# Scratch layout of the split state-space operands: one write of each half, and loads that repeat rows

## The chip, the cores and the metric

The kernel runs on one core of a Trainium2 chip. The metric is the device time of one launch in microseconds (us); before the change it is 2741.55 us, the median of 3 runs (2741.41 to 2743.21). PE is the matrix engine, DVE the vector engine, ACT the scalar engine, POOL the GpSimd engine, SP the engine that issues the weight transfers.

## The reference, cut to what matters

A trunk of two layers over 256 tokens of width 2048, all in float32. Each layer has a mixer (differential attention beside a state-space branch, both gated) and an MLP. The change touches only the input side of the state-space branch:

```
u   = x @ w_in[:, OFF_U:OFF_GA]                      # (256, 1024): 64 groups of 16 channels
z   = (exp(dt a) - 1) / a                            # complex, per group and state
bb  = z * b                                          # (64 groups, 64 states, 16 channels), complex
bu  = einsum('blgh,gph->blgp', u, bb)                # re and im
s_t = exp(dt a) s_(t-1) + bu_t                       # scanned over the 256 tokens
y   = Re(c s) + d u, then GELU, then a sigmoid GLU
```

The kernel moves z to the output side (into c), so that the product it forms is u with the plain b.

## The kernel before, in words

**Weights.** All large products have the weights streamed: SP issues one transfer of 512 KB for each chunk of 256 rows (line 344, four buffers for the raw data). ACT rounds the chunk to the upper part `whi` (line 142) and DVE forms the rest `wlo` (line 144), three buffers each. PE multiplies in float32r and sums three products: upper by upper, upper by lower, lower by upper (lines 532 to 534 for the projections, 457 to 461 for products by token, 555 for the MLP's first half).

**The state-space branch in the background.** `ssm_gen` (line 643) is a generator of small steps that are put between the chunks of the large products; a scheduler then sets the order on each engine from its own estimate of durations. The product bu is made in 32 steps, 16 a layer (4 groups g of feature tiles, 4 steps k each). Every step takes one tile `bs` (weights: upper and lower part of b) and one tile `us` (upper and lower part of u), both with a single buffer, and issues 4 matmuls into `bu` (line 685), 128 states by 256 tokens each. u is in the order of its channels, and a step needs the channels of one pair of groups on 96 partitions: 32 rows, three times, so that one matmul with 96 rows sums upper by upper, lower by upper and upper by lower. This regrouping goes through memory:

- `b_gen` (line 572) loads the raw b (`braw`, line 577), splits it into `hi` and `lo` for each of four g, and writes each part to the scratch tensor `bsplit`: three writes of 256 KB per g (hi, lo, hi again; line 590), 12 a layer.
- `u_evac` (line 927) runs four times a layer, after each half of the two u products; it splits its two feature tiles and writes three parts to `usplit` (hi, hi, lo; line 934), 256 KB each, 12 a layer.
- `operands(i)` (line 657) loads `bs` and `us` of step i (lines 662 and 664), 192 KB each. It is called right after the matmuls of step i-1, whose reading frees the two buffers.

All of these transfers are issued by POOL, in order. A write takes 128 partitions of 2 KB; its target is a view of three dimensions, 4 blocks of 32 rows, since each part has its own place between the blocks. Other POOL transfers of the same size (`emem`, `xkeep`, `lnb`, `cz`) have 128 rows as the first dimension on both sides.

After the bu matmuls, DVE multiplies by the powers e (lines 692 to 698), scans (line 710), and PE forms y (line 731).

Of the kernel before, what the change touches and what calls it, by code (L numbers as in the profile page):

```python
# [11 lines left out]
F32 = mybir.dt.float32  # L12
F32R = mybir.dt.float32r
# [7 lines left out]
P = 128  # L21
# [9 lines left out]
L = 64  # L31
# [73 lines left out]
def trunk(ctx: ExitStack, tc: tile.TileContext, A, out):  # L105
# [13 lines left out]
    def nm(s):  # L119
        uid[0] += 1  # L120
        return f"{s}_{uid[0]}"

    def slot(shape, dt=F32, name="slot"):
        return slots.tile(shape, dt, tag="slot", name=nm(name))
# [447 lines left out]
    def b_gen(l):  # L572


        raw = slot([P, 4, 2, 256], name="braw")
        for g in range(4):
            hold(GP.dma_start(raw[:, g], A["bT"][l][:, g]))
            yield 0.3
        if l == 0:
            yield from ssm_param_gen()  # L580
        else:
            yield 2.0
        bsplit[l] = dram.tile([4, 4, 3, 32, 2, 256], F32, tag=f"bsplit{l}", name=f"bsplit{l}")
        hi, lo = (slot([P, 4, 2, 256], name="bhl") for _ in range(2))
        for g in range(4):
            h = SC.activation(hi[:, g].bitcast(F32R), raw[:, g], AF.Copy)
            hold(h)
            V.tensor_tensor(lo[:, g].bitcast(F32R), raw[:, g], hi[:, g], op=ALU.subtract)
            for m, t in enumerate((hi, lo, hi)):
                GP.dma_start(bsplit[l][g, :, m], t[:, g])  # L590
            yield 0.6

    def e_steps(l, g, im, re, hold=lambda i: i):
        jj = slice(l * 32 + 8 * g, l * 32 + 8 * g + 8)
# [48 lines left out]
    def ssm_gen(l, st):  # L643
        lp = l * 32
        e_re = slot([P, 4, 8, L], name="e_re")
        e_im = slot([P, 4, 8, L], name="e_im")
        w = [slot([P, NCH, 8, L], name="sw") for _ in range(2)]
        for g in range(4):
            if l in emem:
                for t, e in zip((e_re, e_im), emem[l]):  # L650
                    drip.append((t[:, g], e[:, g]))
            else:
                for step in e_steps(l, g, e_im[:, g], e_re[:, g]):
                    yield 0.1 if isinstance(step, tuple) else step
        while st["u"] is None:
            yield 0.5
        def operands(i):
            if i == 16:
                return None
            g, h, kk = i // 4, i // 2 % 2, i % 2  # L660
            bs = tmp.tile([96, 2, 2, P], F32, tag="bs", name=nm("bs"), bufs=1)
            GP.dma_start(bs.rearrange("p q c s -> p q (c s)"), bsplit[l][g, 2 * kk:2 * kk + 2, :, :, h].rearrange("q m r s -> (m r) q s"))
            us = tmp.tile([96, 2, 256], F32, tag="us", name=nm("us"), bufs=1)
            GP.dma_start(us, st["split"][2 * kk:2 * kk + 2, :, :, 2 * g + h].rearrange("q m r t -> (m r) q t"))
            return bs, us

        nxt = operands(0)
        uT = st["u"]
        for g in range(4):
            jj = slice(lp + 8 * g, lp + 8 * g + 8)  # L670
            cz = tmp.tile([P, 2, 8, 32], F32, tag="cz", name=nm("cz"), bufs=2)
            GP.dma_start(cz, cmem[l][g] if l in cmem else A["cT"][l, g])
            rt = t_bg([P, 8, L])
            SC.activation(rt, s_r[:, jj, None].broadcast_to([P, 8, L]), AF.Copy)
            GP.memset(rt[:, :, 0:1], 0.0)
            yield 0.1
            if l not in cmem:
                c_steps(l, g, cz)
                yield 2.0
            for k in range(4):  # L680
                bs, us = nxt
                bu = psa.tile([P, 2, 2, NCH, L], F32, tag="bu", name=nm("bu"), bufs=1)
                for q in range(2):
                    for ri in range(2):
                        PE.matmul(bu[:, q, ri].rearrange("p a b -> p (a b)"), bs[:, q, ri, :].bitcast(F32R), us[:, q, :].bitcast(F32R), start=True, stop=True)
                nxt = operands(4 * g + k + 1)
                yield 0.3
                er = e_re[:, g, 2 * k:2 * k + 2, None, :].broadcast_to([P, 2, NCH, L])
                ei = e_im[:, g, 2 * k:2 * k + 2, None, :].broadcast_to([P, 2, NCH, L])
                wr, wi = (w[ri][:, :, 2 * k:2 * k + 2, :].rearrange("p c q t -> p q c t") for ri in range(2))  # L690
                ta, tb = t_bg([P, 2, NCH, L]), t_bg([P, 2, NCH, L])
                V.tensor_tensor(wr, bu[:, :, 0], er, op=ALU.mult)
                V.tensor_tensor(ta, bu[:, :, 1], ei, op=ALU.mult)
                V.tensor_tensor(wi, bu[:, :, 1], er, op=ALU.mult)
                yield 1.8
                V.tensor_tensor(tb, bu[:, :, 0], ei, op=ALU.mult)
                V.tensor_tensor(wr, wr, ta, op=ALU.add)
                V.tensor_tensor(wi, wi, tb, op=ALU.subtract)
                yield 1.8
            rg = rt.rearrange("p a b -> p (a b)")  # L700
            er, ei = e_re[:, g], e_im[:, g]
            carry = None
            for c in range(NCH):
                if c > 0:
                    for ri in range(2):
                        V.tensor_tensor(carry[:, ri, :], carry[:, ri, :], s_r[:, lp + 8 * g:lp + 8 * g + 8], op=ALU.mult)
                        V.tensor_tensor(w[ri][:, c, :, 0], w[ri][:, c, :, 0], carry[:, ri, :], op=ALU.add)
                for ri in range(2):
                    wv = w[ri][:, c].rearrange("p a b -> p (a b)")
                    V.tensor_tensor_scan(wv, rg, wv, 0.0, ALU.mult, ALU.add)  # L710
                yield 2.4
                s = [w[0][:, c], w[1][:, c]]
                ta, tb, td = t_bg([P, 8, L]), t_bg([P, 8, L]), t_bg([P, 8, L])
                V.tensor_tensor(ta, s[1], ei, op=ALU.mult)
                V.tensor_tensor(tb, s[0], ei, op=ALU.mult)
                V.tensor_tensor(td, s[0], er, op=ALU.mult)
                yield 1.8
                V.tensor_tensor(s[1], s[1], er, op=ALU.mult)
                V.tensor_tensor(s[0], td, ta, op=ALU.subtract)
                V.tensor_tensor(s[1], s[1], tb, op=ALU.add)  # L720
                if c < NCH - 1:
                    carry = sm([P, 2, 8], tag="carry", bufs=2)
                    for ri in range(2):
                        V.tensor_copy(carry[:, ri, :], s[ri][:, :, L - 1])
                yield 1.8
            yps = psa.tile([P, 2, 2, 256], F32, tag="bu", name=nm("y"), bufs=1)[:, 0]
            mm = [Chain() for _ in range(4)]
            for h in range(2):
                for ri in range(2):
                    for j in range(4):  # L730
                        mm[j](PE.matmul(yps[32 * j:32 * j + 32, h, :], cz[:, ri, 4 * h + j, :], w[ri][:, :, 4 * h + j, :],
                                        start=ri == 0, stop=ri == 1, tile_position=(0, 32 * j)))
            yield 0.3
            y, a = t_bg([P, 2, 256]), t_bg([P, 2, 256])
            uc = uT[:, 2 * g:2 * g + 2, :]
            for k in range(2):
                SC.activation(y[:, k, :], uc[:, k, :], AF.Copy, scale=dsk[:, l, 2 * g + k:2 * g + k + 1])
            V.tensor_tensor(y, yps, y, op=ALU.add)
            SC.activation(a, y, AF.Square, scale=math.sqrt(GELU_C))
            yield 0.7  # L740
            V.scalar_tensor_tensor(a, a, 1.0, y, op0=ALU.add, op1=ALU.mult)
            SC.activation(a, a, AF.Tanh, scale=GELU_K)
            yield 0.7
            V.scalar_tensor_tensor(uc, a, 1.0, y, op0=ALU.add, op1=ALU.mult)
            yield 0.6
# [165 lines left out]
    for l in range(DEPTH):  # L911
# [9 lines left out]
        sgen = early()  # L921
        first = False
        uT = slot([P, 8, 256], name="uT")
        uhl = [slot([P, 8, 256], name="uhl") for _ in range(2)]
        st["split"] = dram.tile([4, 3, 32, 8, 256], F32, tag=f"usplit{l}", name=f"usplit{l}")

        def u_evac(b, ps):
            ct = 4 * n + 2 * b
            u = uT[:, ct:ct + 2, :]
            hi, lo = (t[:, ct:ct + 2, :] for t in uhl)  # L930
            SC.activation(u, ps, AF.Copy)
            split(hi.bitcast(F32R), lo.bitcast(F32R), u)
            for m, t in enumerate((hi, hi, lo)):
                GP.dma_start(st["split"][:, m, :, ct:ct + 2], t)

        rate[0] = RATE[l]
        bg.add(sgen)
# [237 lines left out]
```

## Time and profile before

| | |
|---|---|
| median of 3 runs | 2741.55 us |
| the profiled execution's own time | 2731.09 us |
| its span, first to last instruction | 2729.3 us |
| PE busy | 2676.5 us (98%) |
| DVE busy | 1908.7 us (70%) |
| ACT busy | 1312.6 us (48%) |
| POOL busy | 147.1 us (5%) |
| moved by SP's queue | 482.40 MB, 53.2% of the 16 DMA engines' span |
| moved by POOL's queue | 50.99 MB, 6.6% |
| mean granted TensorE clock | 0.994 |

The profile gives each engine's busy time and, for each group of instructions, the idle time before them and what ended it. A wait of PE's in the chain adds to the span; idle time of an engine that nobody waits for adds nothing. For transfers it gives the time from the issue to the landing. The 53.2% and 6.6% are shares of what the 16 DMA engines could do over the whole span, a mean over stretches that differ.

### The profile page before, as it was taken

Reading aid. Unit: us, or ns where it says so; the run is one execution under the profiler, and the core shown is the slowest. Engines: PE = TensorE matmul, PEld = TensorE weight load, DVE = VectorE, ACT = ScalarE, POOL = GpSimd, SP = SyncE. Lnnn points to the kernel's source line nnn. Section 1 sums busy time; section 2 is a strip of 40 time slices with the busy share of each in tenths; the row PEclk is TensorE's granted clock in tenths of the full one; section 3 lists DMA queues with packets and bytes.
Section 4 is the critical chain, followed back from the end, with each engine's and each line's share of the span. In section 5 each row is a group of like instructions: output and inputs, shape, how many; then the busy total and the mean of one; then the engine's idle time right before and its main releaser. Section 6 shows DMA issues by size and latency. Waiting matters only on the chain. (4 is left out here: it accounts for less than half of the span.)

```text
span 2729.3 us, 41597 instructions
## 1 busy us (share of the span) xinstructions
PE 2676.5 (98%) x16384; PEld 2371.8 (87%) x16384; DVE 1908.7 (70%) x2675; ACT 1312.6 (48%) x1755; POOL 147.1 (5%) x274
## 2 busy tenths in 40 slices
PE   7999999999999999999999999999999999999997
PEld 7889999988888888888789899999788888888876
DVE  6899988676765566655657998987776655556555
ACT  4554555454554454443444555544445544435442
POOL 3100000000000010000012000001000000000000
PEclk9999999999999999999999999999999999999999
DMA  8755555663655676655657555557746555555573
GB/s 262 224 187 188 174 173 169 212 234 122 220 190 192 205 237 212 220 198 195 227 167 253 185 179 171 166 179 230 252 135 205 187 194 191 190 195 186 193 234 121
DMA packets 158675, 536.04 MB, mean 196 GB/s; under 512 B 27504, under 2 KB 27536, under 8 KB 158480
## 3 DMA queue, kind: packets, MB, share of 16 engines
q1 hardware_dynamic: 133344, 482.40, 53.2%
q0 software_dynamic: 25136, 50.99, 6.6%
q8 instruction: 128, 2.10, 0.3%
q14 instruction: 67, 0.55, 0.1%
HBM read 513.32 MB, written 19.92 MB: 195 GB/s over the span
## 5 line engine op out<-in xcount | busy, mean ns | idle before, releaser
L144 DVE TENSOR_TENSOR wlo<-w,whi 128x1024 fp32r<-128x1024 f32 (+1 forms) x884 | 1078.3, 1221 | 660.3 <-ACT whi L142 655.3
L142 ACT ACTIVATE whi<-w 128x1024 fp32r<-128x1024 f32 (+1 forms) x884 | 934.3, 1058 | 1085.3 <-PE g L461 425.6
L555 PE MATMUL g<-xT,whi 128*128 128x512 f32 x1920 | 655.7, 395 | 2.3 <-ACT whi L142 2.3
L532 PE MATMUL g<-xT,whi 128*128 128x256 f32 x1792 | 509.3, 287 | 11.8 <-ACT whi L142 11.8
L533 PE MATMUL g<-xT,whi 128*128 128x256 f32 x1792 | 508.5, 286 | 0.0
L534 PE MATMUL g<-xT,wlo 128*128 128x256 f32 x1792 | 500.0, 287 | 7.1 <-DVE wlo L144 7.0
L555 PE MATMUL g<-xT,wlo 128*128 128x256 f32 x1920 | 497.7, 280 | 0.2 <-DVE wlo L144 0.2
L555 PEld LDWEIGHTS g<-xT,whi 128*128 128x128 f32 x1920 | 344.9, 188 | 66.9 <-ACT whi L142 2.6
L458 PE MATMUL g<-wlo,hT 128*128 128x512 f32 x972 | 379.4, 390 | 3.6 <-DVE wlo L144 3.5
L555 PEld LDWEIGHTS g<-xT,wlo 128*128 128x128 f32 x1920 | 362.1, 189 | 21.7 <-DVE wlo L144 1.4
L457 PE MATMUL g<-whi,hT 128*128 128x512 f32 x972 | 379.1, 390 | 0.9 <-ACT whi L142 0.9
L532 PEld LDWEIGHTS g<-xT,whi 128*128 128x128 f32 x1792 | 347.9, 194 | 14.7 <-ACT whi L142 12.9
L534 PEld LDWEIGHTS g<-xT,wlo 128*128 128x128 f32 x1792 | 341.8, 194 | 10.2 <-DVE wlo L144 9.6
L533 PEld LDWEIGHTS g<-xT,whi 128*128 128x128 f32 x1792 | 347.9, 194 | 1.0 <-issue 0.8
L461 PE MATMUL g<-whi,hT 128*128 128x512 f32 x972 | 300.3, 390 | 0.0
L458 PEld LDWEIGHTS g<-wlo,hT 128*128 128x128 f32 x972 | 182.7, 188 | 43.9 <-DVE wlo L144 5.7
L457 PEld LDWEIGHTS g<-whi,hT 128*128 128x128 f32 x972 | 182.9, 188 | 39.6 <-ACT whi L142 2.1
L461 PEld LDWEIGHTS g<-whi,hT 128*128 128x128 f32 x972 | 182.9, 188 | 38.0
L458 PE MATMUL g<-wlo,merged 128*128 128x512 f32 x216 | 85.3, 395 | 3.4 <-DVE wlo L144 3.2
L560 ACT ACTIVATE at<-g 128x256 f32<-128x256 f32 x120 | 43.8, 384 | 87.3 <-PE g L555 87.3
L457 PE MATMUL g<-whi,merged 128*128 128x512 f32 x216 | 84.4, 391 | 0.0
L710 DVE TENSOR_TENSOR_SCAN sw<-ss,sw 128x512 f32<-128x512 f32 x64 | 75.7, 1212 | 0.0
(290 smaller groups left out, 3186.1 us busy)
## 6 DMA issues: line engine op xcount, KB each, us to landing
w<-in_w_mlp_down_dram SPq DMA_DIRECT2D x256, 512.0 KB, 3.3
w<-in_w_in_dram SPq DMA_DIRECT2D x255, 512.0 KB, 3.4
w<-in_w_mlp_up_dram SPq DMA_DIRECT2D x240, 512.0 KB, 3.3
w<-in_w_out_dram SPq DMA_DIRECT2D x64, 512.0 KB, 4.3
w<-in_w_attn_up_dram SPq DMA_DIRECT2D x32, 512.0 KB, 3.3
w<-in_w_ssm_up_dram SPq DMA_DIRECT2D x32, 512.0 KB, 4.3
w<-in_w_glu_dram SPq DMA_DIRECT2D x16, 512.0 KB, 3.2
w<-in_w_mlp_head_dram SPq DMA_DIRECT2D x16, 512.0 KB, 3.5
```

The source lines that it names most:

```text
L142: SC.activation(hi, src, AF.Copy, scale=scale)
L144: V.tensor_tensor(lo, src, hi.bitcast(F32), op=ALU.subtract)
L457: mm(PE.matmul(ps[tt], act(kt)[:, 0, ts], hi[:, k, :], start=kt == 0, stop=False))
L458: mm(PE.matmul(ps[tt], act(kt)[:, 0, ts], lo[:, k, :], start=False, stop=False))
L461: mm(PE.matmul(ps[tt], act(kt)[:, 1, ts], hi[:, k, :], start=False, stop=kt == nkt - 1))
L532: m(PE.matmul(o, wh, ah, start=first and b % 2 == 0, stop=False))
L533: m(PE.matmul(o, wh, al, start=False, stop=False))
L534: m(PE.matmul(o, wl, ah, start=False, stop=last and b % 2 == 1))
L555: mm[j](PE.matmul(o, wt, mv, start=kt == 0 and i == 0, stop=last and i == 1))
L560: SC.activation(r[:, j], ps[j][:, 0, :], AF.Copy)
L710: V.tensor_tensor_scan(wv, rg, wv, 0.0, ALU.mult, ALU.add)
```

## The change

Each part of b and of u is now written once. Two groups g of b share one tile and one write of 1 MB (2 a layer), and each of the two u products ends in one write of 1 MB. The scratch tensors have the two parts of a row side by side: 4 blocks, 32 rows, 2 parts, and then 8 KB less the parts, so that a write is 128 rows of 8 KB that follow each other. A step's operands are now one block j of 32 rows, both parts: 64 rows. The load of `bs` takes these 64 rows twice (a first dimension of 2 that repeats), the load of `us` takes each row twice, in two transfers, one for each part. So a step has 128 partitions with four products (lower by lower too), 256 KB each of `bs` and `us`, three loads in place of two; the two feature tiles that a step yields are now k and k+4 in place of 2k and 2k+1.

```diff
@@ b_gen
-        bsplit[l] = dram.tile([4, 4, 3, 32, 2, 256], F32, tag=f"bsplit{l}", name=f"bsplit{l}")
-        hi, lo = (slot([P, 4, 2, 256], name="bhl") for _ in range(2))
-        for g in range(4):
-            h = SC.activation(hi[:, g].bitcast(F32R), raw[:, g], AF.Copy)
-            hold(h)
-            V.tensor_tensor(lo[:, g].bitcast(F32R), raw[:, g], hi[:, g], op=ALU.subtract)
-            for m, t in enumerate((hi, lo, hi)):
-                GP.dma_start(bsplit[l][g, :, m], t[:, g])
-            yield 0.6
+        bsplit[l] = [dram.tile([4, 32, 2, 2, 2, 256], F32, tag=f"bsplit{l}{i}", name=f"bsplit{l}{i}") for i in range(2)]
+        for i in range(2):
+            hl = slot([P, 2, 2, 2, 256], name="bhl")
+            for k in range(2):
+                hold(SC.activation(hl[:, 0, k].bitcast(F32R), raw[:, 2 * i + k], AF.Copy))
+                V.tensor_tensor(hl[:, 1, k].bitcast(F32R), raw[:, 2 * i + k], hl[:, 0, k], op=ALU.subtract)
+                yield 0.6
+            GP.dma_start(bsplit[l][i].rearrange("j r m k h c -> (j r) (m k h c)"), hl.rearrange("p m k h c -> p (m k h c)"))
@@ operands
-            g, h, kk = i // 4, i // 2 % 2, i % 2
-            bs = tmp.tile([96, 2, 2, P], F32, tag="bs", name=nm("bs"), bufs=1)
-            GP.dma_start(bs.rearrange("p q c s -> p q (c s)"), bsplit[l][g, 2 * kk:2 * kk + 2, :, :, h].rearrange("q m r s -> (m r) q s"))
-            us = tmp.tile([96, 2, 256], F32, tag="us", name=nm("us"), bufs=1)
-            GP.dma_start(us, st["split"][2 * kk:2 * kk + 2, :, :, 2 * g + h].rearrange("q m r t -> (m r) q t"))
+            g, j = i // 4, i % 4
+            bs = tmp.tile([P, 2, 2, P], F32, tag="bs", name=nm("bs"), bufs=1)
+            us = tmp.tile([P, 2, 256], F32, tag="us", name=nm("us"), bufs=1)
+            b = bsplit[l][g // 2][j, :, :, g % 2].rearrange("r m h c -> (r m) (h c)")
+            GP.dma_start(bs.rearrange("p h c s -> p (h c s)"), b[None].broadcast_to([2, 64, 512]))
+            for m in range(2):
+                u = st["split"][g // 2][j, :, m, 2 * (g % 2):2 * (g % 2) + 2].rearrange("r h t -> r (h t)")
+                GP.dma_start(us[64 * m:64 * m + 64].rearrange("p h t -> p (h t)"), u[:, None].broadcast_to([32, 2, 512]))
@@ the step's first DVE operations
-                er = e_re[:, g, 2 * k:2 * k + 2, None, :].broadcast_to([P, 2, NCH, L])
-                ei = e_im[:, g, 2 * k:2 * k + 2, None, :].broadcast_to([P, 2, NCH, L])
-                wr, wi = (w[ri][:, :, 2 * k:2 * k + 2, :].rearrange("p c q t -> p q c t") for ri in range(2))
+                er = e_re[:, g, k::4, None, :].broadcast_to([P, 2, NCH, L])
+                ei = e_im[:, g, k::4, None, :].broadcast_to([P, 2, NCH, L])
+                wr, wi = (w[ri][:, :, k::4, :].rearrange("p c q t -> p q c t") for ri in range(2))
@@ u_evac and its tiles
-        uhl = [slot([P, 8, 256], name="uhl") for _ in range(2)]
-        st["split"] = dram.tile([4, 3, 32, 8, 256], F32, tag=f"usplit{l}", name=f"usplit{l}")
+        uhl = [slot([P, 2, 4, 256], name="uhl") for _ in range(2)]
+        st["split"] = [dram.tile([4, 32, 2, 4, 256], F32, tag=f"usplit{l}{i}", name=f"usplit{l}{i}") for i in range(2)]
...
-            hi, lo = (t[:, ct:ct + 2, :] for t in uhl)
+            hi, lo = (uhl[n][:, m, 2 * b:2 * b + 2] for m in range(2))
...
-            for m, t in enumerate((hi, hi, lo)):
-                GP.dma_start(st["split"][:, m, :, ct:ct + 2], t)
+            if b == 1:
+                GP.dma_start(st["split"][n].rearrange("j r m c t -> (j r) (m c t)"), uhl[n].rearrange("p m c t -> p (m c t)"))
```

The scheduler places the instructions anew. The rows below stand in the built programs, engine by engine; the line numbers of the changed kernel are one less or two more than those of the kernel before. The last part of a row is the shape of what is written.

POOL in layer 0, at the loads of the first two steps. Before:

```order
L590 DMA bsplit_506<-bhl_508 4x32x512
L662 DMA bs_881<-bsplit_506 96x2x256
L590 DMA bsplit_506<-bhl_508 4x32x512
L664 DMA us_883<-usplit_170 96x2x256
L934 DMA usplit_170<-uhl_168 4x32x512 x4
L934 DMA usplit_170<-uhl_169 4x32x512 x2
L662 DMA bs_933<-bsplit_506 96x2x256
L664 DMA us_935<-usplit_170 96x2x256
```

Now, from the first write of b (the first write of u stands right ahead of it):

```order
L590 DMA bsplit_507<-bhl_509 128x2048
L590 DMA bsplit_508<-bhl_554 128x2048
L666 DMA us_864<-usplit_170 64x1x512 x2
L663 DMA bs_863<-bsplit_507 128x1x512
L663 DMA bs_916<-bsplit_507 128x1x512
L666 DMA us_917<-usplit_170 64x1x512 x2
L936 DMA usplit_171<-uhl_169 128x2048
```

Ahead of the first step's last load there stood 18 writes (12 of b, 6 of u); there stand 3 now. The second half of u was written between the loads of the two steps and is written behind both now.

PE in layer 0, about the first bu matmuls (`g` is a large product; rows with xT_118 are the first chunk of the product after u, with xT_141 a later one). Before:

```order
L532 MATMUL g_849<-xT_141,whi_944 128x256
L533 MATMUL g_849<-xT_141,whi_944 128x256
L532 MATMUL g_850<-xT_141,whi_944 128x256
L533 MATMUL g_850<-xT_141,whi_944 128x256
L685 MATMUL bu_928<-us_883,bs_881 128x256 x4
L534 MATMUL g_849<-xT_141,wlo_945 128x256
```

Now:

```order
L534 MATMUL g_520<-xT_163,wlo_750 128x256
L532 MATMUL g_831<-xT_118,whi_788 128x256
L533 MATMUL g_831<-xT_118,whi_788 128x256
L532 MATMUL g_832<-xT_118,whi_788 128x256
L533 MATMUL g_832<-xT_118,whi_788 128x256
L687 MATMUL bu_911<-us_864,bs_863 128x256 x4
L534 MATMUL g_831<-xT_118,wlo_789 128x256
```

The first bu matmuls stood behind 76 matmuls of the product after u; they stand behind 4 now, 72 matmuls earlier.

POOL in layer 1, about the first write of u (`xkeep` is the residual, put aside). Before:

```order
L447 DMA xkeep<-x_6005 128x512
L934 DMA usplit_12946<-uhl_12944 4x32x512 x2
L934 DMA usplit_12946<-uhl_12945 4x32x512 x2
L447 DMA xkeep<-x_6005 128x512 x3
L664 DMA us_13856<-usplit_12946 96x2x256
L447 DMA xkeep<-x_6006 128x512 x4
L934 DMA usplit_12946<-uhl_12944 4x32x512 x4
```

Now:

```order
L447 DMA xkeep<-x_6003 128x512
L936 DMA usplit_12935<-uhl_12933 128x2048
L447 DMA xkeep<-x_6003 128x512 x2
L666 DMA us_13835<-usplit_12935 64x1x512 x2
L447 DMA xkeep<-x_6003 128x512
L447 DMA xkeep<-x_6004 128x512 x4
L663 DMA bs_13849<-bsplit_9753 128x1x512
```

One write stands where six stood ahead of the first load of `us`, and the second write of u is behind the loads of the second step here too.

In PE's row, the other matmuls between the bu matmuls of one step and of the next number, for steps 1 to 15 of layer 0: before 159, 33, 72, 499, 64, 29, 30, 413, 90, 54, 53, 478, 89, 58, 50; now 226, 38, 72, 499, 64, 29, 36, 414, 96, 60, 56, 477, 85, 63, 55. For steps 17 to 31 of layer 1: before 106, 66, 48, 579, 47, 29, 48, 458, 86, 136, 51, 458, 74, 56, 56; now 59, 82, 59, 540, 50, 13, 36, 499, 135, 123, 60, 465, 57, 59, 61. (Steps are counted from 0; the counts take single matmuls of whatever width.)

## Rows read from the trace of the kernel before

**Rows 1.** Page, part 1: busy us (share of the span) xinstructions.

```profile
PE 2676.5 (98%) x16384; PEld 2371.8 (87%) x16384; DVE 1908.7 (70%) x2675; ACT 1312.6 (48%) x1755; POOL 147.1 (5%) x274
```

**Rows 2.** Windows: start:end, length, busy by engine, PE clock, DMA share, GB/s.

```profile
200.00:300.00 100.00, 100.00 (x741) 91.91 (x740) 93.56 (x167) 51.12 (x97) 8.33 (x14) 1.00 0.57 185
300.00:400.00 100.00, 100.00 (x819) 94.87 (x818) 91.52 (x163) 49.87 (x91) 5.20 (x9) 1.00 0.53 174
```

**Rows 3.** Waits from 40 to 100 us, those of PE: total, times, longest.

```profile
PE bu L685 <- DMA us<-usplit: 5.0, 1, 5.0
...
PE g L532 <- ACT whi L142: 3.9, 1, 3.9
...
PE g L534 <- DVE wlo L144: 1.9, 3, 0.9
```

**Rows 4.** Waits of PE from 900 to 1500 us.

```profile
PE g L555 <- ACT whi L142: 2.3, 1, 2.3
PE bu L685 <- DMA us<-usplit: 1.4, 2, 1.3
```

**Rows 5.** Windows of 5 us, in the order of engines of rows 2.

```profile
60.00:65.00 5.00, 0.91 (x4) 0.50 (x2) 1.05 (x1) 1.80 (x2) 1.87 (x4) 0.75 0.97 308
65.00:70.00 5.00, 4.77 (x25) 4.78 (x26) 4.08 (x10) 2.99 (x5) 2.02 (x3) 0.57 0.95 250
```

**Rows 6.** Timeline of POOL, layer 0: start, us, what, idle before and its end.

```profile
68.13 0.67 POOL L662 DMA_DIRECT2D bs<-bsplit  x1 [0.92 <-DMA usplit<-uhl]
...
73.51 0.67 POOL L664 DMA_DIRECT2D us<-usplit  x1 [1.62 <-DMA bsplit<-bhl]
```

**Rows 7.** Page of transfers: issues, KB each, median us from issue to landing.

```profile
bsplit<-bhl POOLq DMA_DIRECT2D x24, 256.0 KB, 12.7
usplit<-uhl POOLq DMA_DIRECT2D x24, 256.0 KB, 12.9
bs<-bsplit POOLq DMA_DIRECT2D x32, 192.0 KB, 3.8
...
emem<-ss POOLq DMA_DIRECT2D x8, 256.0 KB, 4.7
...
e_re<-emem POOLq DMA_DIRECT2D x4, 256.0 KB, 4.0
```

**Rows 8.** The tile bhl: landing of the writes of b.

```profile
DMA to landing us min/median/max: 7.0/12.7/18.3
```

**Rows 9.** Narrow windows after the first bsplit write of layer 1, and of emem writes.

```profile
953.90:954.40 0.50, 0.50 (x5) 0.41 (x4) 0.14 (x2) 0.42 (x2) 0.35 (x1) 1.00 0.43 26
990.00:990.50 0.50, 0.50 (x4) 0.40 (x3) 0.00 (x0) 0.50 (x2) 0.12 (x1) 0.50 1.09 344
990.50:991.00 0.50, 0.50 (x3) 0.40 (x3) 0.00 (x0) 0.50 (x1) 0.22 (x1) 0.61 0.94 377
```

**Rows 10.** Timeline of POOL at steps 5 to 7 of layer 0.

```profile
205.07 0.64 POOL L662 DMA_DIRECT2D bs<-bsplit  x1 [13.88 <-PE bu L685]
205.71 0.64 POOL L664 DMA_DIRECT2D us<-usplit  x1
212.15 0.64 POOL L662 DMA_DIRECT2D bs<-bsplit  x1 [5.81 <-PE bu L685]
```

**Rows 11.** Timeline of PE there, and the pace of matmuls with 512 columns.

```profile
211.21 0.64 PE L685 MATMUL bu<-us,bs 96*128 96x256 f32 x4
211.69 0.40 PE L458 MATMUL g<-wlo,xT 128*128 128x512 f32 x1
211.93 0.40 PE L457 MATMUL g<-whi,xT 128*128 128x512 f32 x1
...
218.08 0.72 PE L685 MATMUL bu<-us,bs 96*128 96x256 f32 x4
```

**Rows 12.** Timeline of PE: the pace of matmuls with 256 columns.

```profile
20.09 0.28 PE L534 MATMUL g<-xT,wlo 128*128 128x256 f32 x1
20.21 0.28 PE L532 MATMUL g<-xT,whi 128*128 128x256 f32 x1
```

## The prediction

> **What bounds the kernel now.** I read the page's busy times first: PE is busy for 98% of the span [rows 1], so a change gains only what PE waits, and loses whatever it makes PE wait. The windows say where the other engines come near: from 200 to 400 us, where the steps of the state-space branch run, PE is busy throughout, DVE for 92 to 94%, and the DMA engines for 53 to 57%, nearly all of it weights [rows 2]. There PE has no wait left that could cover a new one. Next come PE's waits. Between 40 and 100 us it waits 10.8 us: 5.0 us, once, for the load of `us`, and 3.9 and 1.9 us for weights that are split late [rows 3]. In layer 1, from 900 to 1500 us, it waits 2.3 us for a late weight and 1.4 us for `us` [rows 4]. A wait costs more than its length: with PE's wait of 3.9 us the granted clock is 0.75 and then 0.57 in the two windows from 60 us [rows 5], means of stretches at 2.4 and at 1.2 GHz, and that is (0.25 + 0.43) x 5 = 3.4 us of PE's pace. The first loads of operands are late because POOL's row is full of writes: `bs` goes out at 68.1 us and `us` at 73.5, after waits for earlier writes [rows 6].
>
> **The writes.** They are slow now. The median landing is 12.7 and 12.9 us, though others of this size that have 128 rows first on both sides, `emem`, take 4.7 [rows 7]; the best write of b still takes 7.0 [rows 8], so a crowded queue is not all of it. The narrow windows show the difference: just after the first write of b in layer 1 the engines move 26 GB/s at a share of 0.43; with two writes of `emem` and the weights they move 344 and 377 GB/s [rows 9]. I read this as the shape: a transfer whose one side leads with a dimension of 4 runs on few of the 16 engines. One engine moves 377 / (16 x 0.94) = 25 GB/s [rows 9], so 256 KB take 2.6 us on four engines and 0.65 us on sixteen.
>
> The change removes 48 such writes, 12.6 MB, and adds 8 of 1 MB, 8.4 MB, with 128 rows first on both sides. A 1 MB write is not in the trace: at the 377 GB/s of rows 9 it takes 2.8 us, at the pace of a crowded `bsplit` write it would take four times 12.7 us. I take it near the first, since the form is that of `emem`. What this gives is bounded by PE's waits where writes run. In layer 0 these are the 10.8 us of rows 3 and, for its two long waits, twice 3.4 us of clock; in layer 1 the 3.7 us of rows 4 and, if each of two places costs half of what rows 5 show, 3.4 us: 25 us at most, and 0 at least. I take 8. In layer 0 the first bu matmuls now stand 72 matmuls earlier, 8.6 us at 0.12 us each [rows 12]; three writes of 1 MB and then the loads still stand ahead of them, so PE waits there again: 4 us of gain. In layer 1 one write replaces six ahead of the first load: 4 us.
>
> **The loads.** This is where I expect the change to lose. Each of 32 steps loads `bs` and `us` right after the bu matmuls of the step before, and PE needs both at the next bu. One step from the rows: bu ends at 211.85 us, `bs` is issued at 212.15, `us` 0.64 later (as at 205.07 and 205.71) [rows 10], each lands about 3.8 us after its issue [rows 7], and the next bu comes at 218.08 [rows 11]. PE's own work between them is 6.2 us, the loads need some 4.7. They are hidden by 1.5 us.
>
> The new load of `bs` takes 256 KB, and its source leads with a dimension of 2, the repetition. No row shows a load of that kind. The lower bound is that it runs as `e_re`, 256 KB with 128 rows first, in 4.0 us [rows 7]. The nearest row in kind is the write that leads with 4. By the same reading the new load runs on two engines: 256 KB at 50 GB/s take 5.2 us where 192 KB on sixteen take 0.5, so it lands 3.8 - 0.5 + 5.2 = 8.5 us after its issue, 8.8 after the end of bu. That is with the two engines to itself. The weights hold half of each engine [rows 2]; if they do so throughout, 5.2 becomes 10.4 and the landing 14 us after bu. They stop when PE stops, since their buffers fill, so I take **10 us**, nearer to the lower of the two. The two loads of `us` (0.64 us more on POOL) lead with 64 and 32 rows and come behind it.
>
> The Trainium skill has a rule for this (DMA: Bandwidth & Descriptors, "Rules for kernel authors", use all 16 engines): a DMA is confined by the slowest dimension of its two patterns, and it names a leading repetition of c copies, which leaves at most c engines. The writes of rows 8 and 9 agree with it, and no run here shows a repeated load yet. By it the sum below stands; by the row of `e_re` it would be that of the first rival.
>
> PE's work between two bu's, from the counts in the changed order at 0.12 us for 256 columns and 0.23 for 512 [rows 11, 12], is below 9 us in 17 steps: 4.7, 8.9, 6.7, 7.6, 7.3, 6.8, 7.8, 6.6 in layer 0 and 7.3, 7.3, 8.7, 3.0, 8.3, 7.5, 7.1, 7.3, 7.7 in layer 1, 120.6 us in all. (The scheduler has put up to 0.7 us more between them than before; it knows of a third load.) The other 15 have 10 us or more. With 10 us for the load, PE waits 17 x 10 - 120.6 = **49 us**. Bounds: at 8.8 us 29, at 14 us 117 and 10 more in four longer steps.
>
> The lower clock comes on top. Within a group of steps the slower work fills the next wait; after a group's last step it is lost: 8 groups at about 2 us, **16 us** (between half of the 3.4 us of rows 5 and a little less than all).
>
> **What is free.** The bu matmuls have 128 rows where they had 96, and the same 256 columns; even 0.12 us more for each step [rows 12] would be 4 us. The strided views k::4 leave DVE's runs of 64 as they are. The second write of u waits behind the second step's loads, but only steps 8 to 15 read it, over 100 us later.
>
> **The sum.** 49 + 16 - 8 = 57 us more. On the profiled execution, 2731.1 us, that is 2788; the median of the runs is 10.5 us above that execution, so the forecast is 2741.5 + 57 = **2798 us**.
>
> **Rivals.** *All 16 engines for the load.* A repeated source may be laid out by its 128 target rows. Then `bs` lands 4 to 4.5 us after its issue and the third load 0.64 us later, 5.6 after bu: only the steps with 4.7 and 3.0 us wait, 3.5 us together, the writes' gain stays, and the stretches at 40 to 90 us may give more than 8: 2741.5 + 3.5 - 12 = 2733 us, between 2720 and 2742. It decides at a landing of about 7 us after bu, where the five shortest steps wait 7 us and eat up the gain. For it: all present loads are quick [rows 7], and none of them is slow by its form. Against it: the writes are slow by theirs. [...] *The load is slow, but less so than the step is long.* At 7 to 7.5 us after bu the waits come to 7 to 12 us, the gain to 8: 2741 to 2747 us, no change. That needs a load that is faster than two engines at the pace of rows 9. *The weights suffer too.* Each load of `bs` holds two engines, and each weight transfer needs all of them; if the weights were late as between 40 and 70 us [rows 3], PE would wait beyond the loads: 2 us in each of 32 steps more, 2860 us. Four raw buffers stand against it.
>
> **How the numbers follow.** I give 0.70 to the slow load (the last rival is its upper end), 0.20 to all engines, 0.10 to no change. Within the slow load, 8.8 us gives 29 + 8 - 8 = 29, some 2770 us, and a larger gain of the writes 2755; the upper bound gives 127 + 20 - 8, 2880. The range must hold 8 in 10: from 2734 us, which takes in the middle case and part of the fast one, to 2860; some 2 in 10 lie outside, most of them below. The likeliest case alone lies between 2755 and 2860. A measurement tells 0.2%, 5.5 us: faster than that 0.18, within it 0.12, slower 0.70.
>
> **What would show it.** The median landing of `bs` in the new profile: 8 us or more if right, about 4.5 if wrong. PE's wait for `bs` or `us` at bu: some 50 us in 17 or so places, against 5.0 and 1.4 us now [rows 3, 4]. The clock below 1.00 in windows from 200 to 400 us, where it was 1.00. Writes of 1 MB that land in less than 10 us, and no wait of PE above 2 us for weights between 40 and 70 us. The forecast is wrong if the load lands before 7 us after bu.

## The result, and the profile after

The changed kernel takes **2812.8 us**, the median of 4 runs (2808.06 to 2816.19), against 2741.5 us (4 runs, 2739.34 to 2743.21): a ratio of 1.0259, 95% interval 1.0242 to 1.0277. It is slower by 71 us. The forecast was 2798 us in a range of 2734 to 2860, slower at 0.70. The direction, the place and the mechanism held. Two terms of the sum were too small, and since their signs differ, much of the error cancelled: the writes give three times what the prediction took, and the loads cost half as much again.

The profiled execution took 2816.19 us, with a span of 2814.4 us and a mean clock of 0.983 (before 2729.3 us and 0.994). First the page's busy times and DMA packets:

```profile
PE 2697.1 (96%) x16384; PEld 2389.0 (85%) x16384; DVE 1913.8 (68%) x2675; ACT 1311.1 (47%) x1755; POOL 138.2 (5%) x266
...
DMA packets 162643, 536.08 MB, mean 190 GB/s; under 512 B 32496, under 2 KB 32528, under 8 KB 161424
```

PE is busy 20.6 us longer than in [rows 1] with the same 16384 matmuls, and the span is 85 us longer, so some 64 us are new waits. PE's waits over the whole program (total, times, longest) show them:

```profile
PE bu L687 <- DMA us<-usplit: 66.8, 18, 8.6
PE bu L687 <- DMA bs<-bsplit: 8.3, 1, 8.3
PE g L458 <- DVE wlo L144: 7.9, 11, 1.5
PE g L532 <- ACT whi L142: 7.3, 3, 5.6
PE g L534 <- DVE wlo L144: 7.2, 8, 1.9
```

At bu PE now waits 75.1 us in 19 places; in [rows 3, 4] it was 5.0 and 1.4 us. The waits for split weights (lines 457, 458, 532, 534 and 555) come to 25 us in all, before to 29. The transfers, issue to landing, answer to [rows 7]:

```profile
us<-usplit POOLq DMA_DIRECT2D x64, 128.0 KB, 9.4
bs<-bsplit POOLq DMA_DIRECT2D x32, 256.0 KB, 9.2
...
usplit<-uhl POOLq DMA_DIRECT2D x4, 1024.0 KB, 10.2
bsplit<-bhl POOLq DMA_DIRECT2D x4, 1024.0 KB, 8.4
```

The loads of a step land more than twice as late, those of `us` too, though their own form is wide. One step in the timelines, POOL's and then PE's (start, us, what, idle before and its end), the counterpart of [rows 10, 11]:

```profile
224.08 0.82 POOL L663 DMA_DIRECT2D bs<-bsplit  x1 [12.47 <-PE bu L687]
224.89 1.08 POOL L666 DMA_DIRECT2D us<-usplit  x2
```

```profile
222.59 1.19 PE L687 MATMUL bu<-us,bs 128*128 128x256 f32 x4 [6.58 <-DMA us<-usplit]
223.58 0.63 PE L458 MATMUL g<-wlo,xT 128*128 128x512 f32 x1
...
227.70 0.39 PE L458 MATMUL g<-wlo,xT 128*128 128x512 f32 x1
...
236.18 0.73 PE L687 MATMUL bu<-us,bs 128*128 128x256 f32 x4 [3.21 <-DMA us<-usplit]
```

The first bu waited 6.58 us. A matmul of 512 columns takes 0.63 us behind it and 0.39 us a little later: the clock had fallen and came back. The next bu comes 12.4 us after the end of the first, again behind a wait. The windows (columns as in [rows 2]) give the clock:

```profile
200.00:300.00 100.00, 90.21 (x608) 79.48 (x607) 82.04 (x145) 42.74 (x79) 8.26 (x14) 0.95 0.55 169
300.00:400.00 100.00, 91.46 (x712) 87.21 (x711) 77.64 (x138) 45.17 (x88) 6.54 (x11) 0.93 0.49 155
```

```profile
220.00:225.00 5.00, 2.41 (x8) 2.15 (x9) 1.19 (x2) 0.00 (x0) 0.92 (x2) 0.50 0.08 31
```

PE was busy 100% at 1.00 in the first two windows before [rows 2]. In the 5 us around the wait at 222 us PE is at 0.50, that is 1.2 GHz, and the DMA engines move only 31 GB/s at a share of 0.08: 0.10 MB of weights and 0.04 MB on POOL's queue, that of the operands. In the next window, behind another step, POOL's queue moves data alone:

```profile
329.00:329.50 0.50, 0.50 (x6) 0.50 (x6) 0.50 (x2) 0.00 (x0) 0.00 (x0) 1.00 0.13 49
```

A share of 0.13 is two engines of 16, and 49 GB/s is twice the 25 GB/s that the prediction took for one engine from [rows 9]: the operands of one step, whose `bs` was issued at 322.19 us, are still being loaded, on two engines.

### The profile page after: what moved, and what is told of

Its sections match the earlier page's. It is cut to its first block, busy times and chain, and to the rows that moved or that the text cites. A ratio compares the mean times of both kernels' runs of the same rounds, so it can differ in the third digit from the quotient of the medians.

```text
span 2814.4 us, 41598 instructions
## 1 busy us (share of the span) xinstructions
PE 2697.1 (96%) x16384; PEld 2389.0 (85%) x16384; DVE 1913.8 (68%) x2675; ACT 1311.1 (47%) x1755; POOL 138.2 (5%) x266
## 2 busy tenths in 40 slices
DMA packets 162643, 536.08 MB, mean 190 GB/s; under 512 B 32496, under 2 KB 32528, under 8 KB 161424
## 5 line engine op out<-in xcount | busy, mean ns | idle before, releaser
L534 PEld LDWEIGHTS g<-xT,wlo 128*128 128x128 f32 x1792 | 346.5, 197 | 11.3 <-DVE wlo L144 8.8
L687 PE MATMUL bu<-us,bs 128*128 128x256 f32 x128 | 28.3, 351 | 75.9 <-DMA us<-usplit 66.8
L687 PEld LDWEIGHTS bu<-us,bs 128*128 128x128 f32 x128 | 22.2, 238 | 80.6 <-issue 79.3
```

Of the source, the lines that this page charges most:

```text
L534: m(PE.matmul(o, wl, ah, start=False, stop=last and b % 2 == 1))
```

## The experiments

My theory: a transfer whose one side leads with a small dimension runs on that many engines; so the new load of `bs` runs on two, and the old writes on four. The rivals were the bytes, the number of loads, the repetition itself, the scheduler's new order, and the number of writes.

**The load in two halves, without the repetition.**

```diff
-            GP.dma_start(bs.rearrange("p h c s -> p (h c s)"), b[None].broadcast_to([2, 64, 512]))
+            for m in range(2):
+                GP.dma_start(bs[64 * m:64 * m + 64].rearrange("p h c s -> p (h c s)"), b)
```

> The load of bs is made by two transfers of 64 rows each, in place of one whose source leads with a repetition of 2. The bytes are the same, a step has four loads in place of three, and the writes are those of the changed kernel. Theory, the leading 2 keeps the transfer on two engines: bs lands 3 to 4.5 us after its issue (9.2 us in the changed kernel), PE's wait at bu falls from 75 us to below 12 us, and the time is 2725 to 2745 us. Rival, it is the bytes (256 KB where 192 KB were) or the number of loads of a step: bs lands 7 us or more after its issue, and the time stays above 2790 us. Rival, the cost lies in where the scheduler put the new work: the loads are quick, and the time still stays above 2780 us.

Measured: 2715.5 us (2712.73 to 2716.22), ratio to before 0.9905 (0.989 to 0.992). Waits and issues:

```profile
PE bu L688 <- DMA us<-usplit: 2.0, 2, 1.1
...
PE bu L688 <- DMA bs<-bsplit: 1.0, 1, 1.0
```

```profile
us<-usplit POOLq DMA_DIRECT2D x64, 128.0 KB, 4.3
bs<-bsplit POOLq DMA_DIRECT2D x64, 128.0 KB, 3.8
```

One line turns 71 us slower into 24 us faster (2739.7 us for before in the same series). The bytes are as in the changed kernel and a step has one load more, so those rivals fall. PE's order isn't the same: the scheduler put more matmuls between some steps (41 between steps 5 and 6, where 29 stood), so the rival of the new order falls only with the next run, where PE's matmuls stand in the order of the changed kernel. The time is below the 2725 to 2745 us I expected: the gain on the other side was larger than I thought.

**The repetition inside.**

```diff
-            GP.dma_start(bs.rearrange("p h c s -> p (h c s)"), b[None].broadcast_to([2, 64, 512]))
+            GP.dma_start(bs.rearrange("p h c s -> p (h c s)"), b[:, None].broadcast_to([64, 2, 512]))
...
-                GP.dma_start(us[64 * m:64 * m + 64].rearrange("p h t -> p (h t)"), u[:, None].broadcast_to([32, 2, 512]))
+                GP.dma_start(us[m::2].rearrange("p h t -> p (h t)"), u[:, None].broadcast_to([32, 2, 512]))
```

> The load of bs stays one transfer of 256 KB with repeated rows, but each row is repeated in place, so that its source leads with 64 rows and the repetition of 2 stands second; the loads of us go to every second partition to match. Three loads a step and the same bytes as in the changed kernel. Theory, the leading 2 is the cause: bs lands within 4.5 us of its issue, PE's wait at bu falls below 10 us, and the time is 2722 to 2740 us, that of the first rival of the prediction. Rival, a repeated source is slow wherever the repetition stands: bs lands in 8 us or more, and the time stays near 2812 us. Rival, the granted clock is lower for the whole program (more rows in the bu matmuls): the waits go and the time still stays above 2760 us, with a mean clock below 0.99.

Measured: 2713.7 us (2713.03 to 2715.21), ratio 0.990 (0.9883 to 0.9916), below the range I gave.

```profile
PE 2666.6 (98%) x16384; PEld 2363.9 (87%) x16384; DVE 1910.6 (70%) x2675; ACT 1311.2 (48%) x1755; POOL 130.1 (5%) x266
...
DMA packets 148307, 535.96 MB, mean 198 GB/s; under 512 B 18160, under 2 KB 18192, under 8 KB 147088
```

```profile
PE bu L687 <- DMA us<-usplit: 3.8, 3, 2.0
```

```profile
us<-usplit POOLq DMA_DIRECT2D x64, 128.0 KB, 3.8
bs<-bsplit POOLq DMA_DIRECT2D x32, 256.0 KB, 3.9
...
usplit<-uhl POOLq DMA_DIRECT2D x4, 1024.0 KB, 6.3
bsplit<-bhl POOLq DMA_DIRECT2D x4, 1024.0 KB, 6.0
```

The same bytes with the same rows read twice land in 3.9 us in place of 9.2. A repetition is not slow; a leading 2 is. This kernel against the changed one prices the load's form: 2812.8 - 2713.7 = 99 us. In the two profiles it is 71.3 us of waits at bu (75.1 - 3.8) and 30.5 us of longer PE work (2697.1 - 2666.6), together 101.8, and the spans differ by 101.0.

**A leading 2 without a repetition.**

```diff
+            b = bsplit[l][g // 2][j % 2::2, :, :, g % 2].rearrange("j r m h c -> j (r m) (h c)")
-            GP.dma_start(bs.rearrange("p h c s -> p (h c s)"), b[None].broadcast_to([2, 64, 512]))
+            GP.dma_start(bs.rearrange("p h c s -> p (h c s)"), b)
```

> The load of bs has no repetition: its source leads with 2, two different blocks of 64 rows each, everything else as in the changed kernel. It reads rows of another block for half of the partitions, so the product bu isn't formed from the right rows of b; the instructions and the bytes are the same. Theory, the leading dimension of 2 counts, repeated or not: bs lands in 8 to 11 us, PE's wait at bu is 60 to 90 us, the time 2795 to 2830 us. Rival, the repetition is what is slow (the same rows of memory read twice at a time): bs lands within 5 us, and the time falls to 2725 to 2750 us.

Measured: 2815.2 us (one run). It is as slow as the changed kernel, with the same waits:

```profile
PE bu L688 <- DMA us<-usplit: 68.5, 16, 9.0
PE bu L688 <- DMA bs<-bsplit: 8.5, 1, 8.5
```

```profile
bs<-bsplit POOLq DMA_DIRECT2D x32, 256.0 KB, 9.8
```

**The dose.** The source of `bs` is cut into 2, 4, 8 or 16 pieces, by turns.

```diff
+            wide = (2, 4, 8, 16)[(i + g) % 4]
...
-            GP.dma_start(bs.rearrange("p h c s -> p (h c s)"), b[None].broadcast_to([2, 64, 512]))
+            b = bsplit[l][g // 2][:, :, :, g % 2].rearrange("j r m h c -> (j r m) (h c)")
+            b = b.rearrange("(a q) x -> a q x", a=wide if wide > 2 else 4)
+            b = b[:, :128 // wide] if wide > 2 else b[j % 2::2, :64]
+            GP.dma_start(bs.rearrange("p h c s -> p (h c s)"), b)
```

> The steps take turns: the source of bs leads with 2, 4, 8 or 16 pieces of 64, 32, 16 or 8 rows (tiles bsa, bsb, bsc, bsd, eight loads each), 256 KB in all of them. Rows of other blocks are read, so bu isn't formed from the right rows of b. Theory, so many engines as the leading dimension has: the part of the landing that goes with the bytes halves with each step, so that median landings are about 9.2, 6, 4.5 and 4 us, and PE's wait at bu is 20 to 30 us (mostly at the steps with bsa), the time 2755 to 2785 us. Rival, one penalty for anything below 16: bsa, bsb and bsc all land in 8 us or more and bsd in 4. Rival, no matter of the leading dimension: all four within 1 us of each other.

Measured: 2762.2 us (one run).

```profile
bsa<-bsplit POOLq DMA_DIRECT2D x8, 256.0 KB, 11.5
bsb<-bsplit POOLq DMA_DIRECT2D x8, 256.0 KB, 6.7
bsc<-bsplit POOLq DMA_DIRECT2D x8, 256.0 KB, 5.1
bsd<-bsplit POOLq DMA_DIRECT2D x8, 256.0 KB, 4.4
```

Each doubling of the leading dimension takes off 4.8, 1.6 and 0.7 us, at least halved each time. At 25 GB/s for each engine [rows 9] the bytes would give 2.6, 1.3 and 0.65: the last two fit, the first is larger. The shortest of the eight landings of each (9.1, 6.3, 4.5 and 4.0 us) differ by 2.8, 1.8 and 0.5; the median of `bsa` holds loads of up to 18.9 us, and why isn't shown. The rivals (one penalty, or none) fall. The waits at bu were 42.6 us in 12 places, more than the 20 to 30 expected.

**Narrow writes.** The version with the repetition inside, its eight large writes (four a layer) made to lead with 4.

```diff
-        bsplit[l] = [dram.tile([4, 32, 2, 2, 2, 256], F32, tag=f"bsplit{l}{i}", name=f"bsplit{l}{i}") for i in range(2)]
+        bsplit[l] = [dram.tile([4, 33, 2, 2, 2, 256], F32, tag=f"bsplit{l}{i}", name=f"bsplit{l}{i}")[:, :32] for i in range(2)]
...
-            GP.dma_start(bsplit[l][i].rearrange("j r m k h c -> (j r) (m k h c)"), hl.rearrange("p m k h c -> p (m k h c)"))
+            GP.dma_start(bsplit[l][i].rearrange("j r m k h c -> j r (m k h c)"), hl.rearrange("p m k h c -> p (m k h c)"))
```

The same two edits are made for `usplit`.

> The version with the repetition inside (2713.7 us), with the scratch blocks padded to 33 rows, so that the four 1 MB writes of a layer lead with 4 as the writes of the kernel before did; loads and number of writes as in that version. Theory, the form of the writes gives the gain: the 1 MB writes land in 13 us or more (median of tiles bhl and uhl, 6.0 and 6.3 us with 128 rows first), PE waits again in the first 100 us, and the time is 2722 to 2745 us. Rival, the gain comes from fewer writes and fewer bytes: the time stays within 2710 to 2718 us although the writes land late.

Measured: 2761.3 us (2758.33 to 2765.34), ratio 1.0076 (1.0056 to 1.0097). Waits of PE, then the writes:

```profile
PE g L532 <- ACT whi L142: 20.1, 4, 12.6
PE bu L687 <- DMA us<-usplit: 11.9, 3, 5.7
...
PE bu L687 <- DMA bs<-bsplit: 4.1, 1, 4.1
```

```profile
usplit<-uhl POOLq DMA_DIRECT2D x4, 1024.0 KB, 20.1
bsplit<-bhl POOLq DMA_DIRECT2D x4, 1024.0 KB, 26.0
```

The form of eight writes costs 47.6 us (2761.3 - 2713.7), more than I expected, and a split weight comes up to 12.6 us late. Two windows of 3.5 us in which POOL's queue alone moves data, the first three large writes, here wide (the version with the repetition inside) and then narrow:

```profile
46.50:50.00 3.50, 2.50 (x21) 2.30 (x20) 3.50 (x6) 1.06 (x1) 0.53 (x1) 1.00 0.97 386
```

```profile
52.00:55.50 3.50, 3.50 (x32) 3.50 (x31) 3.50 (x8) 0.32 (x1) 0.00 (x0) 1.00 0.67 103
```

The weights suffer. Those issued from 40 to 60 us land after 22.1 us, with the wide writes after 8.7 and in the kernel before after 13.7 (medians of five to seven transfers):

```profile
w<-in_w_in_dram SPq DMA_DIRECT2D x5, 512.0 KB, 22.1
```

Fewer and larger writes bring nothing by themselves: with eight narrow ones the kernel is slower than the kernel before with its 48 (2740.7 us).

**The kernel before with wide writes only.** The parts of a row side by side; nothing else changes, and PE's matmuls stand in the same order.

```diff
-        bsplit[l] = dram.tile([4, 4, 3, 32, 2, 256], F32, tag=f"bsplit{l}", name=f"bsplit{l}")
+        bsplit[l] = dram.tile([4, 4, 32, 3, 2, 256], F32, tag=f"bsplit{l}", name=f"bsplit{l}")
...
-                GP.dma_start(bsplit[l][g, :, m], t[:, g])
+                GP.dma_start(bsplit[l][g, :, :, m].rearrange("q r h c -> (q r) (h c)"), t[:, g].rearrange("p h c -> p (h c)"))
...
-        st["split"] = dram.tile([4, 3, 32, 8, 256], F32, tag=f"usplit{l}", name=f"usplit{l}")
+        st["split"] = dram.tile([4, 32, 3, 8, 256], F32, tag=f"usplit{l}", name=f"usplit{l}")
```

The write of `usplit` is folded to 128 rows in the same way, and the loads take `(r m)` for `(m r)`.

> The kernel before with one edit: the three parts of a row lie side by side in the scratch tensors, so that each of its 48 writes of 256 KB is 128 rows of 2 KB and leads with 128 in place of 4. Same number of writes, same bytes, same places in the order, the same loads of 96 partitions. Theory, the form of the writes: they land in 4 to 7 us (12.7 and 12.9 before), PE's waits between 40 and 100 us fall from 10.8 to below 4 us, and the time is 2712 to 2728 us, most of the gain of the version with the repetition inside. Rival, number and bytes of the writes: they still land in 10 us or more, or land sooner and the time stays above 2732 us.

Measured: **2706.9 us** (2705.24 to 2708.31), ratio 0.9878 (0.9856 to 0.9899), the fastest of all.

```profile
bsplit<-bhl POOLq DMA_DIRECT2D x24, 256.0 KB, 5.8
usplit<-uhl POOLq DMA_DIRECT2D x24, 256.0 KB, 6.4
```

The median landing halves, and the waits between 40 and 100 us are down to one:

```profile
PE g L534 <- DVE wlo L144: 0.7, 1, 0.7
```

The kernel before lost 34 us (2740.7 - 2706.9) to the order of two dimensions in its scratch. The rest of the change (fewer writes, 128 rows, a third load) shows no gain beside this: with wide loads it stands at 2713.7 us. The two ratios overlap, so I don't claim that it loses; in the profiles its span is 9.6 us longer, and 3.8 us of that are waits at bu.

**The kernel before, a second profile.** No edit.

> The kernel before, unchanged, with a second profile: its first profiled execution was 10 us shorter than its median. Theory, what differs is the clock after waits: an execution near 2740 us shows more of PE's time at 1.2 GHz and the same waits to within 3 us. Rival, other waits: PE's waits in all are 8 us or more above those of the first profile.

Measured: 2742.98 us. PE's waits at bu, over the whole program and from 40 to 100 us:

```profile
PE bu L685 <- DMA us<-usplit: 19.3, 3, 12.5
```

```profile
PE bu L685 <- DMA us<-usplit: 12.5, 1, 12.5
```

My theory falls and the rival holds. PE is busy 2677.3 us, only 0.8 more than in [rows 1], while the wait for the first `us` is 12.5 us where [rows 3] have 5.0, and at bu PE waits 12.9 us more in all (19.3 against 6.4). The span less PE's busy time is 11.1 us longer (63.9 against 52.8). The prediction's gain was bounded by the waits of an execution that happened to wait little.

**The loads of us first.**

```diff
-            GP.dma_start(bs.rearrange("p h c s -> p (h c s)"), b[None].broadcast_to([2, 64, 512]))
             for m in range(2):
...
+            GP.dma_start(bs.rearrange("p h c s -> p (h c s)"), b[None].broadcast_to([2, 64, 512]))
```

> The changed kernel with the two loads of us issued ahead of the load of bs, which keeps its leading 2. Theory, part of the cost is the loads of us queueing behind the slow bs (they land 9.4 us after their issue, 3.8 where bs is quick, and 2 us behind bs): with us first they land in 3 to 6 us, bs in 8.2 to 9.2, the last operand 10 to 10.5 us after the end of bu in place of 11.5, PE's wait at bu falls from 75 to 50 to 62 us, and the time to 2780 to 2800 us. Rival, the three loads share the engines whatever their order: the last operand lands at 11 to 12 us, and the time stays at 2805 to 2820 us.

Measured: 2800.6 us (2796.79 to 2800.82), ratio 1.0216 (1.0191 to 1.0241). Waits and issues:

```profile
PE bu L687 <- DMA bs<-bsplit: 59.4, 16, 8.2
...
PE bu L687 <- issue: 6.3, 2, 3.7
```

```profile
us<-usplit POOLq DMA_DIRECT2D x64, 128.0 KB, 3.2
bs<-bsplit POOLq DMA_DIRECT2D x32, 256.0 KB, 9.8
```

The loads of `us` had queued behind the slow `bs`: ahead of it they land in 3.2 us, not 9.4. But `bs` then goes out a microsecond later and lands in 9.8. In PE's timeline bu starts 11.6 us after the end of the bu before, in the mean of the 15 waits for `bs` behind the first step (11.3 without one of 15.7), against 11.7 in the 18 for `us` of the changed kernel. So here the rival holds, with 11 to 12 us, and not the theory, with 10 to 10.5. The time is 12 us shorter all the same (2812.8 - 2800.6), just past the weak end of what I expected, and 65.7 us of waits at bu stay. But the scheduler has moved PE's matmuls here too (40 between steps 5 and 6, where 29 stood), and a longer step waits less: how much of the 12 us is the order of the loads isn't shown.

## Why the prediction held, point by point

**What bounds the kernel.** Right. PE had no slack at the steps, and a load later than a step is long went straight into the span.

**The form of the transfers.** Right, and for the loads now shown: 49 GB/s at a share of 0.13 is two engines, and the dose follows the leading dimension. For the writes the form is shown as the cause (wide ones of the same size land in 5.8 and 6.4 us, not 12.7 and 12.9 [rows 7]), four engines are not. The prediction read them out of [rows 9], but 26 GB/s is the pace of one engine and 0.43 the share of seven. Narrow writes of 1 MB run at 103 GB/s, the pace of four engines, yet at a share of 0.67, and three of them were on their way. The Trainium skill's rule (DMA: Bandwidth & Descriptors, "Rules for kernel authors", use all 16 engines) is that an outermost dimension of fewer than 16 keeps a transfer on at most as many engines. These runs agree: `bs` with two in front lands in 9.2 us with the repetition that the rule names and in 9.8 without one, in 3.9 with 64 in front. The Trainium skill's rule of 128 partitions and at least 1 MiB in a transfer for bandwidth (same section) is not enough alone: the narrow writes of 1 MB have 128 partitions too, and with them the kernel takes 2761.3 us.

**The loads, mis-sized: 65 us taken, 99 measured.** `bs` was forecast 8.5 us after its issue with two engines to itself and landed in 9.2, so the load's own price was right. The step that failed is the 10 us taken for the last operand: the two loads of `us` "come behind it", and were given no price. They land behind `bs`, and the last operand is there 11.7 us after bu in the mean of 18 waits (9.9 to 13.2, and 12.4 in the step above); issued ahead of `bs` they hold it up instead, to 11.6 us. With 11.7 for 10 the prediction's own sum gives 17 x 11.7 - 120.6 = 78 us of waits; with 16 us of clock, and 8.3 us of wait at the very first step, which was not among the 17, that is 102 us. So the clock term need not be wrong. In the profiles the cost divides otherwise, 71.3 us of waits and 30.5 us of slower PE work, since inside a group slower work takes the place of waiting, as behind the wait at 222 us, and the prediction had counted that part as wait.

**The writes, mis-sized: 8 us taken, 26 measured** (2739.7 - 2713.7, before and the version with the repetition inside). The step that failed is "PE waits there again: 4 us of gain". In the changed kernel it does wait at the first bu, 8.3 us, but for its own slow load of `bs`; with a wide load 0.5 us are left there. The upper bound, 25 us, came from one profiled execution, 10 us below the median, and the second profile, at the median, shows longer waits. Against that first execution the version with the repetition inside is 15.9 us shorter in its profile (2729.3 - 2713.4), and most of the other 10 us of the 26 are that distance from the median.

**The sum.** 65 - 8 = 57 us were forecast, 99 - 26 = 73 are measured. Of each term a third or more was missing. Their signs differ, so the sum is off by only 16: that it came so near is luck.

**The rivals.** All 16 engines for the load: false for the change as written, and true as soon as the repetition stands inside; its time, 2733 us, was then 19 us too high for the reason just given. The middle case had no chance at a landing of 9.2 us. Weights that suffer too: they land later (from 200 to 300 us after 4.3 us in the median, with the repetition inside after 3.3), but PE doesn't wait longer for them: it waits 7.3 us for `whi` at line 532, and 11.8 in the profile of before.

**The signs.** `bs` landed above 8 us, PE waited at bu in 19 places (75 us, where some 50 were named), the clock fell below 1.00 from 200 to 400 us, and no weight was 2 us late from 40 to 70 us, as named. One sign failed: the 1 MB writes of u landed in 10.2 us, not in less than 10.

**What is free.** Held within what the runs tell apart: 128 rows in the bu matmuls, k::4 and the late second write of u are all in the version at 2713.7 us. Up to the 9.6 us by which its profile is longer than that of the kernel before with wide writes, a cost of theirs isn't excluded.

## What to carry to other kernels

Look at the first dimension of both sides of every transfer before its size or count: fold a row index to the front, and put a repetition or a part index behind it. Such an edit cost nothing here (the kernel before with that edit alone takes 2706.9 us), and a slow transfer whose cause is its form is better mended than avoided. Where a gain is bounded by the waits of one execution that lies off the median, the bound is off by that much too.

## What the runs showed that I had not expected

**The scatter of the times went with the narrow transfers.** Eleven runs of the kernel before lie between 2726.37 and 2746.97 us; six with the same writes made wide between 2705.24 and 2708.31. With eight large narrow writes six runs lie within 7 us, and with narrow loads and wide writes, as in the changed kernel, four within 8 us.

**Narrow loads slow other transfers.** The 1 MB writes have the same form in the changed kernel and in the version with the repetition inside, and land in 10.2 and 8.4 us in the one, in 6.3 and 6.0 in the other.

**Narrow transfers leave a mark on the page.** The changed kernel has 32496 packets under 512 B, the version with the repetition inside 18160, for the same bytes of operands. The difference, 14336, is 32 loads of 448, and 448 is 14 x 32: a whole number for each of the 14 engines that two leave idle. In the dose, whose queue has 20400 packets against 14768 for the version with the repetition inside, the difference of 5632 fits the same way, eight times 14 x 32 + 12 x 16 + 8 x 8:

```profile
q0 software_dynamic: 20400, 50.96, 6.0%
```

```profile
q0 software_dynamic: 14768, 50.91, 5.7%
```

The kernel before and its version with wide writes have 25136 and 15920 packets in this queue; the difference, 9216, is 48 writes of 12 x 16, a whole number for each of the 12 engines that four would leave idle. What these packets are was not tested. As a sign they can be read off a page without an experiment.
